# First-norm stage of a hybrid pool/RG-LRU block: x asked for ahead of its weights, squares spread over the blocks

## The chip, the cores and the metric

The kernel runs on one core of one Trainium2 chip. The metric is the device time of one execution in microseconds (us); lower is better. The engines are named as the profile names them: PE (TensorE; PEld is its weight load), DVE (VectorE), ACT (ScalarE), POOL (GpSimd) and SP (SyncE, which here issues nearly all transfers). Each engine works through its own instruction queue in order, and waits on semaphores that other engines and finished transfers raise.

## What is computed

One layer of a decoder trunk on x (1024 tokens, 1024 channels), float32. What matters for this change is the very first part:

```python
z = rms_norm(h, norm_mix_g[l])          # h is x
proj = z @ w_in[l]                       # 1024 -> 512 pool, 512 lru, 512 gate
u_pool, u_lru, u_gate = split(proj)
xb = causal_depthwise_conv(u_lru, ...)   # then RG-LRU, times gelu(u_gate)
y_pool = multiscale_pool_mixer(u_pool, pool_w, pool_b, pool_scale)
h = h + concat(y_pool, y_lru) @ w_out
...                                      # squared-ReLU MLP, gated per-layer embedding, final norm
```

`rms_norm` is `x * rsqrt(mean(x*x) + eps) * g`. The RG-LRU needs softplus of a parameter vector (`lru_L`), a small side computation.

## The kernel before, in words

Everything is held transposed: channels on the 128 partitions, the 1024 tokens along the free axis. The 1024 channels of x are eight blocks `H[0]` to `H[7]` of 128 x 1024 (512 KB each); in the text, "block k" is the step that treats `H[k]`.

Matrix products are made of float32 values that are split in two float32r parts, hi and lo, so that one product is three matmul passes: hi x hi, hi x lo, lo x hi. The helper `split` (L174) does this with one ACT instruction for hi (L177 without a gain, L180 with the gain of the norm) and one DVE instruction for lo (L178 or L181). The scaling by the inverse root comes after the product (L535), so the product can start before the sum of squares is known.

The change lies in the loop over the eight blocks (L489 to L522). Block k needs:

- its x: a transfer of `H[k]` (L495), and its split into `A[k]` hi and lo (L501, that is L180 on ACT and L181 on DVE);
- its weights: 128 x 384 of `w_lru` (192 KB), the columns of the first three output tiles, transferred into a raw buffer (L195) and split (L177 on ACT, L178 on DVE) by `load_weights`. Here these are called weights k, named `wl` in the profile. Raw, hi and lo buffers come from a pool of two (`wp`, bufs=2), so weights k+2 take the buffers of weights k: their hi part can be written once the last matmul that reads hi of weights k has ended, and their transfer can start once raw of weights k has been split;
- 18 matmuls 128 x 128 x 512 (L521 for blocks 2 to 7): three output tiles, three passes, two halves of the tokens;
- its square on ACT (L387 for the first, L390 for the others) and the addition to the running sum `T[0]` on DVE (L391), by `norm.add`. The squares go to two buffers in turn.

Around the loop stand side works: `tables` (L443, a small table on DVE and the transfers of the gate and pool weights, L452 and L453, 256 KB each) and `softplus` (L459, some 27 DVE instructions on 128 x 4 elements, most of which depend on the one before, and one exponential on ACT, L466). After block 6's matmuls come four matmuls that add up the squares over the partitions (`norm.sums`, L417 and L418), then those of block 7, and then the projections `ps_i`.

What sets the order: the program is written in the order of the source, and a scheduler of the tile framework may move instructions, except those that were pinned. `pin` (L169) pins an instruction to the source's order as long as the list `in_order` is not empty; `split` and `norm.add` pin their instructions. The list is cleared at L509, in block 2. `weights()` (L337) asks for the next weights of a long list (`ask`, L332: transfer and split) and returns the oldest that were asked for. In block 3 one more `ask()` (L492) stands ahead, so from there on the weights are one block ahead: block 4 asks for weights 5, block 5 for weights 6, and so on.

Of the kernel before, what the change touches and what calls it, by code (L numbers as in the profile page):

```python
# [14 lines left out]
S = 1024  # L15
# [7 lines left out]

SOON = 20

AHEAD = ((0,), (1, 2), (3,), ())
IN = {("P5", 2): (0, 1), ("P5", 3): (2, 3), ("P3", 0): (4, 5), ("P3", 1): (6, 7)}
LATER = ((), (0, 1), (2, 3), (4, 5), (6, 7), (), ())
# [29 lines left out]
def block_kernel(  # L58
# [26 lines left out]
    H = [h_all[:, i] for i in range(NT)]  # L85
# [44 lines left out]
    HALVES = FIRST, SECOND = slice(0, HALF), slice(HALF, S)  # L130
# [14 lines left out]
    def f32(ap):  # L145
        return ap.bitcast(F32)
# [16 lines left out]
    def col(name, i):  # L163
        c = COLS[name] + i
        return vecs[:, c : c + 1]
# [3 lines left out]
    def pin(ins):  # L169
        return tc.keep_in_program_order(ins) if in_order else ins  # L170
# [3 lines left out]
    def split(src, hi, lo, g=None, eng=None):  # L174

        if g is None:
            first = pin(nc.scalar.activation(hi, src, AF.Copy))  # L177
            lowest[:] = [pin((eng or nc.vector).tensor_tensor(lo, src, f32(hi), ALU.subtract)).ins]  # L178
        else:
            first = pin(nc.scalar.activation(hi, src, AF.Identity, scale=g))  # L180
            lowest[:] = [pin(nc.vector.scalar_tensor_tensor(lo, src, g, f32(hi), ALU.mult, ALU.subtract)).ins]  # L181
        return first.ins

    def raw_tile(name):
        return wp.tile([P, S], F32, tag="raw", name=f"{name}_raw")

    def weight_tiles(name):
        return [wp.tile([P, S], F32R, tag=f"w{x}", name=f"{name}_{x}") for x in ("hi", "lo")]
# [143 lines left out]
    def ask():  # L332
        if todo:
            fn, *args = todo.pop()
            asked.append(fn(*args))

    def weights():  # L337
        ask()
        return asked.pop(0)

    def mm(parts, whi, wlo, zhi, zlo, first, last, only=None, more=False, held=False):
        outs = [
            (slice(hs.start + n, hs.start + min(n + HALF, w)), ps[:, n : min(n + HALF, w)])
            for hs, ps in parts
            for w in (hs.stop - hs.start,)
            for n in range(0, w, HALF)
            if only is None or hs.start + n == only.start
        ]
        for w, z in ((whi, zhi), (whi, zlo), (wlo, zhi)):
            for hs, ps in outs:  # L350
                ins = nc.tensor.matmul(  # L351
                    ps, w, turns(z[:, hs]),
                    start=first and z is zhi and w is whi,
                    stop=last and w is wlo,
                    skip_group_check=more,
                )
                if held:
                    tc.keep_in_program_order(ins)
                    held = False

    def kblk(t, k):
        return t[:, k * P : (k + 1) * P]
# [80 lines left out]
    def tables():  # L443

        one = ones_f[:, :16]
        tc.keep_in_program_order(
            nc.vector.tensor_tensor_scan(recip_t, one, one, 0.0, ALU.mult, ALU.add)
        )
        nc.vector.reciprocal(recip_t, recip_t)


        nc.sync.dma_start(T[5][:, FIRST], gates)  # L452
        nc.sync.dma_start(T[5][:, SECOND], pool_w)  # L453
# [5 lines left out]
    def softplus():  # L459

        c0 = COLS["lru_l"]
        lv = vecs[:, c0 : c0 + NLRU]
        with tc.issue_after(lowest[0]):
            nc.vector.tensor_scalar_mul(neg, lv, -1.0)
        nc.vector.tensor_tensor(e, lv, neg, ALU.max)
        nc.scalar.activation(e, e, AF.Exp, scale=-1.0)  # L466
        nc.vector.tensor_scalar_add(s, e, 2.0)
        nc.vector.reciprocal(s, s)
        nc.vector.tensor_tensor(s, s, e, ALU.mult)
        nc.vector.tensor_tensor(s2, s, s, ALU.mult)  # L470
        nc.vector.memset(poly, 1.0 / 19)
        for n in range(8, -1, -1):
            nc.vector.tensor_tensor(poly, poly, s2, ALU.mult)
            nc.vector.tensor_scalar_add(poly, poly, 1.0 / (2 * n + 1))
        nc.vector.tensor_tensor(poly, poly, s, ALU.mult)
        nc.vector.tensor_scalar(neg, neg, 0.0, 8.0, ALU.max, ALU.mult)
        nc.vector.scalar_tensor_tensor(cpos, poly, 16.0, neg, ALU.mult, ALU.add)
        nc.vector.tensor_scalar_mul(cneg, cpos, -1.0)

        c_b, c_s = COLS["pool_b"], COLS["pool_s"]  # L480
        with tc.issue_after(lowest[0]):
            nc.vector.tensor_tensor(pool_bs, vecs[:, c_b : c_b + NPOOL], vecs[:, c_s : c_s + NPOOL], ALU.mult)

    norm = Norm("n0", T[0], T[1:3])
# [2 lines left out]
    for _ in range(WARM):  # L487
        nc.tensor.matmul(ps_l[2][0][1][:, :HALF], heat, wide, start=True, stop=True)
    for k in range(NT):  # L489
        if k:  # L490
            if k == 3:
                ask()  # L492
            whi, wlo = weights()
        for hs in HALVES if k < 2 else (slice(0, S),):
            nc.sync.dma_start(H[k][:, hs], xT[k * P : (k + 1) * P, hs])  # L495
            if k == hs.start == 0:
                raw = raw_tile("wl0")[:, : 3 * P]
                whi, wlo = (t[:, : 3 * P] for t in weight_tiles("wl0"))
                nc.sync.dma_start(raw, w_lru[:P, :])
                pin(nc.vector.tensor_copy(whi, raw))  # L500
            split(H[k][:, hs], A[k][0][:, hs], A[k][1][:, hs], col("g_mix", k))  # L501
            if k == hs.start == 0:
                pin(nc.vector.tensor_tensor(wlo, raw, f32(whi), ALU.subtract))
        if k == 2:
            norm.add(H[0])
            norm.add(H[1])
        if k > 1:
            norm.add(H[k])
            in_order.clear()  # L509
        if k == 2:  # L510
            tables()
            softplus()
        if k == NT - 1:
            norm.rstd(R)
        if k < 2:

            for hs in HALVES:
                for o in range(3):
                    mm(ps_l[o], kblk(whi, o), kblk(wlo, o), *A[k], k == 0, False, hs)
            continue  # L520
        for o in range(3):  # L521
            mm(ps_l[o], kblk(whi, o), kblk(wlo, o), *A[k], False, k == NT - 1)  # L522
# [159 lines left out]
    norm = Norm("n1", T[4], T[5:])  # L682
# [66 lines left out]
    def add_got(to, ps, y=None):  # L749

        add(by(to, ps), got(ps), None if y is None else by(y, ps))
# [155 lines left out]
    def prepare(n, tp):  # L907

        if n < NOPS:
            split(X[tp], *A[4 * (n % 2) + tp])  # L910
            load_x(n + 1, tp)
# [19 lines left out]
    def down(n):  # L931
# [6 lines left out]
        for q in range(NQ):  # L938
# [36 lines left out]
            else:  # L975
                add_got(c12, x)
            for tp in AHEAD[q] if n else AHEAD[q - 1]:
                prepare(n + 1, tp)
# [252 lines left out]
```

## Time and profile before

| | |
|---|---|
| time, median of 3 runs (lowest to highest) | 930.12 us (929.95 to 930.37) |
| the profiled execution: time, span | 930.07 us, 928.2 us |
| granted TensorE clock | 0.998 |
| PE busy | 916.3 us (99%) |
| DVE busy | 765.9 us (83%) |
| ACT busy | 457.4 us (49%) |
| POOL busy | 14.9 us (2%) |

The time is what the runs are compared by; the span is the profiled stretch inside it, 1.87 us shorter in this execution. In a row of the timeline the first number is the start in us from the span's start, the second the duration in us, then the engine, the line of the kernel, the operation, output<-input, the shapes and the count (x2: two instructions merged into one row, from the start of the first to the end of the last). Square brackets name the idle time just before and what ended it. SPq is the issue of a transfer on SP's queue, not the transfer itself. Instructions of one engine overlap a little: the next often starts before the end that is shown for the one before, so the distance of two starts is the better price of an instruction in a row of others. Ends of matmuls are modelled.

### The profile page before, as it was taken

To read this page: it belongs to the slowest core of one execution; us is meant where nothing else is said; L and a number is where in the kernel's file an instruction comes from. 1 tells how busy PE (TensorE), PEld (TensorE's weight loads), DVE (VectorE), ACT (ScalarE), POOL (GpSimd) and SP (SyncE) were. 2 spreads that over 40 slices of the span, in tenths; PEclk is the share of its full clock that TensorE was granted. 3 is DMA by queue.
4 is the path that set the end of the run, shared out by engine and by line. 5 is a ranking of instruction groups with operands and counts; after the bars stand their busy time and mean duration, and the time that the engine had idled before them with its cause. 6 is when DMAs were issued, how large, how long until landed. Compare 5 with 4: busy or idle time off the path is not lost.

```text
span 928.2 us, 11481 instructions
## 1 busy us (share of the span) xinstructions
PE 916.3 (99%) x4471; PEld 802.4 (86%) x4471; DVE 765.9 (83%) x930; ACT 457.4 (49%) x545; POOL 14.9 (2%) x11
## 2 busy tenths in 40 slices
PE   9999999999999999999999999999999999999996
PEld 6888888888888888888888888888888888888995
DVE  6997984669998888888888989979776679885976
ACT  7567893447543343343334654434343446653445
POOL 0000000002000000000000000000000000000220
PEclk9999999999999999999999999999999999999999
DMA  7210143211254355345434988366522441031122
GB/s 264 96 50 23 46 154 118 68 45 67 72 189 161 125 175 197 126 148 178 174 125 153 361 314 315 128 209 203 186 91 91 136 136 46 24 117 43 46 92 91
DMA packets 45333, 125.03 MB, mean 135 GB/s; under 512 B 4192, under 2 KB 6240, under 8 KB 45280
## 3 DMA queue, kind: packets, MB, share of 16 engines
q1 hardware_dynamic: 45136, 124.27, 38.4%
q8 instruction: 35, 0.57, 0.3%
q14 instruction: 18, 0.15, 0.1%
q10 hardware_dynamic: 144, 0.04, 0.0%
HBM read 90.74 MB, written 33.55 MB: 134 GB/s over the span
## 4 chain that ended last, share of the span: by engine, by line
PE 91%; DVE 5%; ACT 2%; DMA 1%; issue 0%; DVEq 0%; ACTq 0%
PE ps_P_u L351 31%; PE ps_P_d L351 31%; PE ps_i L351 10%; PE ps_o L351 9%; PE ps_e L351 6%; PE ps_l L351 2%; DVE h L1062 1%; PE ps_j L351 1%; PE ps_g L571 1%; DMA wl_raw<-in_w_lru 1%; DVE h L1079 1%; PE ps_p L351 1%; DVE t L391 1%; DVE t L1061 0%; DVE t L1055 0%; DVE a L178 0%
## 5 line engine op out<-in xcount | busy, mean ns | idle before, releaser
L351 PE MATMUL ps_P_d<-a,wd_P_hi 128*128 128x512 f32 x880 | 261.7, 379 | 0.0
L351 PEld LDWEIGHTS ps_P_d<-a,wd_P_hi 128*128 128x128 f32 x880 | 166.3, 189 | 23.6
L351 PE MATMUL ps_P_d<-a,wd_P_lo 128*128 128x512 f32 x440 | 166.8, 379 | 0.0
L351 PE MATMUL ps_P_u<-a,wu_hi 128*128 128x512 f32 x512 | 152.3, 379 | 0.0
L351 PE MATMUL ps_P_u<-y,wu_hi 128*128 128x512 f32 x384 | 114.2, 379 | 0.0
L351 PEld LDWEIGHTS ps_P_u<-a,wu_hi 128*128 128x128 f32 x512 | 96.8, 189 | 13.8
L351 PE MATMUL ps_P_u<-a,wu_lo 128*128 128x512 f32 x256 | 97.0, 379 | 0.0
L351 PEld LDWEIGHTS ps_P_d<-a,wd_P_lo 128*128 128x128 f32 x440 | 83.2, 189 | 11.8
L351 PEld LDWEIGHTS ps_P_u<-y,wu_hi 128*128 128x128 f32 x384 | 72.6, 189 | 10.3
L747 DVE TENSOR_TENSOR t<-t,ps_P_u 128x512 f32<-128x512 f32 (+1 forms) x80 | 62.6, 783 | 20.4 <-PE ps_P_u L351 20.4
L351 PE MATMUL ps_i<-a,wi_hi 128*128 128x512 f32 x288 | 74.3, 380 | 0.0
L351 PE MATMUL ps_P_u<-y,wu_lo 128*128 128x512 f32 x192 | 72.8, 379 | 0.0
L177 ACT ACTIVATE a<-wd 128x1024 fp32r<-128x1024 f32 x56 | 59.0, 1055 | 21.6 <-PE ps_P_d L351 11.6
L178 DVE TENSOR_TENSOR a<-wd,a 128x1024 fp32r<-128x1024 f32 x56 | 67.4, 1223 | 1.3 <-ACT a L177 0.9
L351 PE MATMUL ps_o<-y,wo_hi 128*128 128x512 f32 x256 | 65.7, 379 | 0.0
L351 PEld LDWEIGHTS ps_i<-a,wi_hi 128*128 128x128 f32 x288 | 54.1, 189 | 8.8 <-issue 0.7
L177 ACT ACTIVATE wu_hi<-wu 128x1024 fp32r<-128x1024 f32 x24 | 25.4, 1059 | 69.8 <-PE ps_P_u L351 44.1
L177 ACT ACTIVATE wu_hi<-wu_raw 128x1024 fp32r<-128x1024 f32 (+1 forms) x26 | 25.3, 976 | 66.3 <-PE ps_P_u L351 41.3
L351 PEld LDWEIGHTS ps_o<-y,wo_hi 128*128 128x128 f32 x256 | 48.4, 189 | 6.8
L351 PEld LDWEIGHTS ps_P_u<-a,wu_lo 128*128 128x128 f32 x256 | 48.4, 189 | 6.8
L177 ACT ACTIVATE wd_P_hi<-wd 128x1024 fp32r<-128x1024 f32 x24 | 25.3, 1055 | 47.3 <-PE ps_P_d L351 47.2
L390 ACT ACTIVATE t<-h 128x512 f32<-128x512 f32 (+2 forms) x47 | 32.8, 699 | 28.9 <-DVE h L1062 20.1
(226 smaller groups left out, 1540.6 us busy)
## 6 DMA issues: line engine op xcount, KB each, us to landing
wd<-act SPq DMA_DIRECT2D x56, 512.0 KB, 5.6
act<-t SPq DMA_DIRECT2D x32, 512.0 KB, 4.3
wu_raw<-in_w_up SPq DMA_DIRECT2D x16, 512.0 KB, 3.2
wu<-in_w_up SPq DMA_DIRECT2D x16, 512.0 KB, 3.8
act<-wu SPq DMA_DIRECT2D x16, 512.0 KB, 4.6
wd<-in_w_down SPq DMA_DIRECT2D x16, 512.0 KB, 6.3
h<-in_xT SPq DMA_DIRECT2D x14, 512.0 KB, 4.5
wg_raw<-in_w_gate SPq DMA_DIRECT2D x12, 512.0 KB, 3.2
```

What stands on the lines that cost most here:

```text
L177: first = pin(nc.scalar.activation(hi, src, AF.Copy))
L178: lowest[:] = [pin((eng or nc.vector).tensor_tensor(lo, src, f32(hi), ALU.subtract)).ins]
L351: ins = nc.tensor.matmul(ps, w, turns(z[:, hs]), start=first and z is zhi and w is whi, stop=last and w is wlo, skip_group_check=more,)
L390: pin(nc.scalar.activation(sq, t[:, hs], AF.Square))
L391: self.eng.tensor_tensor(self.acc[:, hs], self.acc[:, hs], sq, ALU.add)
L571: nc.tensor.matmul(x, w[r, o * P : (o + 1) * P], turns(z[r, at : at + HALF]), start=n == 0, stop=n == 2)
L747: (eng or nc.vector).tensor_tensor(to, to if y is None else y, x, ALU.add)
L1062: nc.vector.tensor_tensor(hv, hv, e, ALU.add)
L1079: nc.vector.scalar_tensor_tensor(hv, hv, col("g_fin", o), rfin[:, hs], ALU.mult, ALU.mult)
```

## The change

In the loop, for blocks 2 to 7, the transfer of `H[k]` is issued ahead of the request for the weights (before, it stood behind it). The additional `ask()` moves from block 3 to block 4. The squares are spread by a table: those of blocks 0 and 1 move behind the splits of blocks 2 and 3, and blocks 4, 5 and 6 add those of blocks 2 and 3, 4 and 5, and 6; block 7 adds its own. The pinned stretch now ends in block 6. `softplus` stays in block 2 but no longer follows `tables`, which moves to block 3, so that the transfers of the gate and pool weights come behind that of the fourth block of x. No arithmetic changes.

```diff
+AFTER = (), (), (0,), (1,), (2, 3), (4, 5), (6,)
...
     for k in range(NT):
-        if k:
-            if k == 3:
-                ask()
+        halves = HALVES if k < 2 else (slice(0, S),)
+        if k == 1:
             whi, wlo = weights()
-        for hs in HALVES if k < 2 else (slice(0, S),):
+        for hs in halves:
             nc.sync.dma_start(H[k][:, hs], xT[k * P : (k + 1) * P, hs])
             if k == hs.start == 0:
                 raw = raw_tile("wl0")[:, : 3 * P]
                 whi, wlo = (t[:, : 3 * P] for t in weight_tiles("wl0"))
                 nc.sync.dma_start(raw, w_lru[:P, :])
                 pin(nc.vector.tensor_copy(whi, raw))
+            if k > 1:
+                if k == 4:
+                    ask()
+                whi, wlo = weights()
             split(H[k][:, hs], A[k][0][:, hs], A[k][1][:, hs], col("g_mix", k))
             if k == hs.start == 0:
                 pin(nc.vector.tensor_tensor(wlo, raw, f32(whi), ALU.subtract))
-        if k == 2:
-            norm.add(H[0])
-            norm.add(H[1])
-        if k > 1:
-            norm.add(H[k])
+        for i in AFTER[k] if k < len(AFTER) else (k,):
+            norm.add(H[i])
+        if k == 6:
             in_order.clear()
         if k == 2:
+            softplus()
+        if k == 3:
             tables()
-            softplus()
         if k == NT - 1:
             norm.rstd(R)
```

## The prediction

> **What bounds the kernel now.** I read the page first (busy shares, chain of waits), then the timeline of each engine over the first 42 us, then the transfers' times to landing. From the page:
>
> ```profile
> span 928.2 us, 11481 instructions
> PE 916.3 (99%) x4471; PEld 802.4 (86%) x4471; DVE 765.9 (83%) x930; ACT 457.4 (49%) x545; POOL 14.9 (2%) x11
> ...
> PE 91%; DVE 5%; ACT 2%; DMA 1%; issue 0%; DVEq 0%; ACTq 0%
> ```
>
> PE is busy 99% of the span and is 91% of the chain. So the change is worth what it does to the moment at which PE ends the block loop: PE has no slack behind it in which a delay could vanish, and an early finish is passed on whole. PE's timeline of the loop:
>
> ```profile
> 1.05 4.02 PE L488 MATMUL ps_l<-heat 128*128 128x512 bf16 x9 [1.05 <-DVE heat L368]
> ...
> 18.01 0.59 PE L351 MATMUL ps_l<-a,wl_hi 128*128 128x512 f32 x2
> 19.36 0.70 PE L351 MATMUL ps_l<-a,wl_hi 128*128 128x512 f32 x2 [0.76 <-DVE a L181]
> ...
> 22.92 1.03 PE L351 MATMUL ps_l<-a,wl_hi 128*128 128x512 f32 x4
> ...
> 26.80 1.03 PE L351 MATMUL ps_l<-a,wl_hi 128*128 128x512 f32 x4
> ...
> 30.69 1.03 PE L351 MATMUL ps_l<-a,wl_hi 128*128 128x512 f32 x4
> ...
> 34.57 0.40 PE L417 MATMUL n_ps<-hl,ones 128*128 128x512 f32 x1
> ...
> 35.51 1.03 PE L351 MATMUL ps_l<-a,wl_hi 128*128 128x512 f32 x4
> ...
> 39.39 1.03 PE L351 MATMUL ps_i<-a,wi_hi 128*128 128x512 f32 x4
> ```
>
> Blocks 3, 4, 5, 6 start at 18.01, 22.92, 26.80 and 30.69, the sums of squares at 34.57, block 7 at 35.51; 39.39 is the end of the loop. A block without a stall takes 3.88 us (22.92 to 26.80), 0.2155 per matmul. There is one stall: block 3 takes 4.91 us, 1.03 too much, because lo of x 3 (DVE L181) came late; 0.76 of it is shown as idle time, the rest is the slower restart. That is all the loop can give back: 0.11% of the time, less than the 0.2% (1.9 us) that a measurement of this kernel can tell from no change.
>
> **The change part by part.** The rows that price it, ACT first, then DVE:
>
> ```profile
> 13.76 1.99 ACT L390 ACTIVATE t<-h 128x1024 f32<-128x1024 f32 x2
> 15.65 0.19 ACT L466 ACTIVATE sp<-sp 128x4 f32<-128x4 f32 x1
> 15.75 0.51 ACT L177 ACTIVATE wl_hi<-wl_raw 128x384 fp32r<-128x384 f32 x1
> 16.16 1.14 ACT L180 ACTIVATE a<-h,vecs 128x1024 fp32r<-128x1024 f32 x1
> 17.21 1.04 ACT L390 ACTIVATE t<-h 128x1024 f32<-128x1024 f32 x1
> 18.16 1.13 ACT L180 ACTIVATE a<-h,vecs 128x1024 fp32r<-128x1024 f32 x1
> ...
> 30.51 0.53 ACT L177 ACTIVATE wl_hi<-wl_raw 128x384 fp32r<-128x384 f32 x1 [2.39 <-PE ps_l L351]
> 34.34 1.06 ACT L177 ACTIVATE wi_hi<-wi_raw 128x1024 fp32r<-128x1024 f32 x1 [3.31 <-PE ps_l L351]
> ```
>
> ```profile
> 14.34 0.16 DVE L465 TENSOR_TENSOR sp<-vecs,sp 128x4 f32<-128x4 f32 x1
> 14.53 0.17 DVE L476 TENSOR_SCALAR sp<-sp 128x4 f32<-128x4 f32 x1
> 14.83 1.23 DVE L391 TENSOR_TENSOR t<-t 128x1024 f32<-128x1024 f32 x1
> 15.98 0.16 DVE L467 TENSOR_SCALAR sp<-sp 128x4 f32<-128x4 f32 x1
> 16.09 1.23 DVE L391 TENSOR_TENSOR t<-t 128x1024 f32<-128x1024 f32 x1
> ...
> 18.03 1.27 DVE L181 SCALAR_TENSOR_TENSOR a<-h,vecs,a 128x1024 fp32r<-128x1024 f32 x1
> 19.22 0.16 DVE L470 TENSOR_TENSOR sp<-sp 128x4 f32<-128x4 f32 x1
> ...
> 20.50 0.55 DVE L178 TENSOR_TENSOR wl_lo<-wl_raw,wl_hi 128x384 fp32r<-128x384 f32 x1
> 20.97 0.17 DVE L474 TENSOR_SCALAR sp<-sp 128x4 f32<-128x4 f32 x1
> ...
> 32.55 0.44 DVE L415 CAST hl<-t 128x512 fp32r<-128x512 f32 x1
> ...
> 33.36 0.70 DVE L416 TENSOR_TENSOR hl<-t,hl 128x512 fp32r<-128x512 f32 x1
> ```
>
> From start to start, ACT takes 0.41 for a weight hi, 1.05 for an x hi, 0.95 for a square; DVE 1.19 for an x lo, 0.47 for a weight lo, 1.26 for an addition behind the one it depends on, 0.19 for a dependent softplus step. All the work stays; only its order changes. In the built program the queues behind block 3 now stand so: ACT: hi of weights 4, x 7, weights 5, x 4, squares 2 and 3, weights 6, x 5, squares 4, 5 and 7, weights 7, x 6, square 6. Before, every x hi stood ahead of the weight hi that waits. Up to block 2's matmuls (end 18.01) nothing moves.
>
> *Block 3.* Two squares leave the place at 13.76, so the exponential starts at 14.55 (behind L465), hi of weights 3 at 14.65, hi of x 3 at 15.07 to 16.20. Its data are there: x 3 is asked for where the gates were (6.21 instead of 9.67, rows below). On DVE five softplus steps from 14.88 on come first, then lo of weights 3 at 15.75, ended 16.31, four more steps, and lo of x 3 at 16.9, ended 18.17. PE needs it at 18.44: the stall goes. Block 3 ends at 21.89. **-1.03 us.**
>
> *Block 4.* ACT's queue has hi of x 7 ahead of weights 5 and x 4, since block 7's split is not pinned and was moved up. It waits for the transfer of x 7, which on SP's queue stands behind that of weights 5, and that waits for lo of weights 3 (16.31). So weights 5, x 6 and x 7 are issued at 16.35, 16.7 and 17.2. The landing times of x before (issue, then the three single transfers of x 4, x 5 and x 7):
>
> ```profile
> 6.21 0.65 SPq L452 DMA_DIRECT2D t<-in_gates  x1
> ...
> 9.67 0.43 SPq L495 DMA_DIRECT2D h<-in_xT  x1
> 12.48 0.33 SPq L195 DMA_DIRECT2D wl_raw<-in_w_lru  x1
> 12.86 1.38 SPq L495 DMA_DIRECT2D h<-in_xT  x3
> ```
>
> ```profile
> h<-in_xT SPq DMA_DIRECT2D x1, 512.0 KB, 4.6
> ```
>
> ```profile
> h<-in_xT SPq DMA_DIRECT2D x1, 512.0 KB, 6.3
> ```
>
> ```profile
> h<-in_xT SPq DMA_DIRECT2D x1, 512.0 KB, 4.8
> ```
>
> The first of the three issued at 12.86 took 4.6, the second 6.3; x 7, almost alone, 4.8. The new x 7 is the second behind a weight transfer, as the 6.3 was, but with no third beside it: I take 5.8, landing at 23.0, with 21.8 and 23.5 as ends. Then hi of x 7 from 23.05, of weights 5 at 24.09, of x 4 from 24.50 to 25.64: PE starts block 4 at 25.70 instead of 21.89. **+3.81.** DVE brings lo of x 7 (24.22), weights 5 (25.41) and x 4 (25.88 to 27.16). PE now runs the six hi x hi matmuls first (25.70 to 27.10 with the restart), waits a trace for lo, and ends at 29.92: **+0.34** over 3.88.
>
> *Block 5.* Its x hi stands behind hi of weights 6, which takes the buffer of weights 4 and waits for block 4's last hi matmul. The rows at 30.51 and 34.34 show when such a wait ends: 0.18 and 0.23 ahead of the next start on PE (30.69, 34.57), say 0.2. So: 29.72, plus 0.41, plus 1.14 for hi of x 5, plus 0.06: PE starts at 31.33, a stall of **1.41**, and **0.11** for the restart (as at 19.36). Its lo (31.31 to 32.6) is ready within the first six matmuls. End: 35.32.
>
> *Block 6.* The same 1.52, and more: ahead of weights 7 stands square 7, which overwrites square 5's buffer. DVE adds square 4 from 32.50 and square 5 from 33.76 to 34.99; square 7 starts at 35.03, hi of weights 7 at 35.98, of x 6 from 36.39 to 37.53. PE starts at 37.59, a stall of **2.27**, plus **0.11**, and ends at 41.58.
>
> *Sums and block 7.* Its x and weights are long there. But the sums need squares 6 and 7 added (DVE 38.8 to 41.3), two casts (0.44) and two lo parts (0.70), between which lo of the next weights stands, and PE's queue has these four matmuls among block 7's. I count three short waits with restarts: **+0.7** (0.2 if the casts win the race, 1.2 if hi of the next weights holds DVE up).
>
> *Behind the loop* the order is nearly the old one; DVE's first scaling (40.50 before) follows PE's loop end by some half us more, which a block's slack hides; if not, it is half a us more. The moved gate and pool transfers are covered: their first reader is the split at the sums. Softplus' end on DVE falls in the wait for x 7.
>
> Sum: -1.03 + 3.81 + 0.34 + 1.52 + 2.38 + 0.7 = **+7.7 us**. On the profiled execution's 930.07 this is 937.8; the median of the runs (930.12) differs by 0.05, which changes nothing.
>
> **The clock.** The nine warm-up matmuls at 1.05 took 0.447 each for the 512 columns that later cost 0.2155: PE starts slow. The idle 0.76 us ahead of 19.36 brought no slow stretch back. [...] The stall ahead of block 4 is forecast at 3.8 us, five times the one seen. If it cools PE, block 4's first nine matmuls cost 9 x 0.23 = 2.1 us more, by the first row.
>
> **The rivals.** (a) *x 7 lands early* (by 20.6): then hi of x 7 fits in ACT's wait for block 3's last hi matmul, block 4 starts at 21.69 + 0.41 + 1.14 + 0.06 = 23.30, 2.4 us sooner: 935.4. For it: fewer bytes are in flight than before at 12.86; against: it would need 3.4 us, and the shortest landing shown for 512 KB of x is 4.6. (b) *PE cools* at block 4: 939.9, as worked out. (c) *Not slower*: the weight buffers come free early enough that x hi of blocks 4 to 6 is ready in time, and only the gain at block 3 is left: 929.0. For it: DVE and ACT have the time, and data arrive earlier. Against: hi of x k stands behind hi of weights k+1 on ACT, and that reads a semaphore that only block k-1's 16th matmul raises. It decides only if x 7, x 4, x 5 and x 6 cost together under 2.9 us of stall; two bounded stalls of 1.5 already use that up.
>
> **How the numbers follow.** Forecast as summed 65% (own range 936.3 to 939.0, from 21.8 to 23.5 for x 7 and the 0.2 to 1.2 of the sums); (a) or between 15%; (b) 12%; (c) 5%; something else 3%. Range 935.0 to 940.2: it leaves out (c) and the tails. Faster by over 0.2%: 1%, since the loop has only 1.03 to give; within 0.2%: 5%, case (c); slower: 94%.
>
> **What would show it.** Right: in the profile after, PE's block 3 without idle time; then idle times of about 3.8, 1.4 and 2.3 us ended by ACT x hi (L181 there), and 46 to 48 us as the start of `ps_i`; ACT idle on the transfer of x once, and on PE ahead of weight hi. Wrong: block 4 starting at 23.3 or earlier, matmuls at 0.43 behind the stall, or no idle time on PE ahead of blocks 5 and 6.

## The result and the profile after

| | before | after |
|---|---|---|
| median (lowest to highest) | 930.04 us (929.83 to 930.37), 4 runs | 938.95 us (938.44 to 941.30), 4 runs |
| the profiled execution: time, span | 930.07 us, 928.2 us | 941.30 us, 939.5 us |
| granted TensorE clock in it | 0.998 | 0.992 |

The ratio is 1.0103, with a 95% interval of 1.0088 to 1.0118: the kernel became slower by 8.9 us. The prediction was 937.8, with a range of 935.0 to 940.2. The profiled execution of after is the slowest of its four, 2.4 us above the median, so a second profiled execution of the same kernel (938.33 us, below called "after, again") is read beside it. The page of after:

```profile
span 939.5 us, 11488 instructions
PE 920.3 (98%) x4471; PEld 804.0 (86%) x4471; DVE 767.7 (82%) x930; ACT 457.4 (49%) x545; POOL 15.2 (2%) x11
```

PE has as many matmuls as before, and four microseconds more of busy time (920.3 against 916.3): work that is the same took longer. The rest of the 11.3 us by which the span grew is idle time. PE's timeline of the block loop shows both (starts in us, duration, and in brackets the idle time ahead and what ended it):

```profile
17.58 1.03 PE L352 MATMUL ps_l<-a,wl_hi 128*128 128x512 f32 x4
...
21.04 0.59 PE L352 MATMUL ps_l<-a,wl_lo 128*128 128x512 f32 x2
26.06 3.78 PE L352 MATMUL ps_l<-a,wl_hi 128*128 128x512 f32 x8 [4.43 <-ACT a L181]
29.64 1.06 PE L352 MATMUL ps_l<-a,wl_lo 128*128 128x512 f32 x2
...
32.10 0.59 PE L352 MATMUL ps_l<-a,wl_lo 128*128 128x512 f32 x2
33.91 2.02 PE L352 MATMUL ps_l<-a,wl_hi 128*128 128x512 f32 x8 [1.22 <-ACT a L181]
...
40.24 2.73 PE L352 MATMUL ps_l<-a,wl_hi 128*128 128x512 f32 x8 [2.15 <-ACT a L181]
...
50.93 1.03 PE L352 MATMUL ps_i<-a,wi_hi 128*128 128x512 f32 x4
```

Block 3 runs without a break from 17.58 to 21.47 (two matmuls behind 21.04, 0.2155 each). Blocks 4, 5 and 6 each begin with an idle time that ACT's hi of x ends. The loop ends at 50.93 where it ended at 39.39. The same eight matmuls that open a block take 2.02 in block 5, but 3.78 in block 4 and 2.73 in block 6. The same places in the timeline of after, again:

```profile
20.60 0.59 PE L352 MATMUL ps_l<-a,wl_lo 128*128 128x512 f32 x2
23.82 2.75 PE L352 MATMUL ps_l<-a,wl_hi 128*128 128x512 f32 x8 [2.63 <-ACT a L181]
...
30.91 2.02 PE L352 MATMUL ps_l<-a,wl_hi 128*128 128x512 f32 x8 [1.22 <-ACT a L181]
...
37.23 2.51 PE L352 MATMUL ps_l<-a,wl_hi 128*128 128x512 f32 x8 [2.15 <-ACT a L181]
...
47.95 1.03 PE L352 MATMUL ps_i<-a,wi_hi 128*128 128x512 f32 x4
```

Here the first stall is 1.8 us shorter. The other two are equal to the hundredth, and the eight slow matmuls in blocks 4 and 6 are there again. ACT's timeline of after says who holds hi of x up:

```profile
17.40 0.52 ACT L178 ACTIVATE wl_hi<-wl_raw 128x384 fp32r<-128x384 f32 x1 [0.71 <-PE ps_l L352]
23.41 1.15 ACT L181 ACTIVATE a<-h,vecs 128x1024 fp32r<-128x1024 f32 x1 [5.49 <-DMA h<-in_xT]
24.46 0.51 ACT L178 ACTIVATE wl_hi<-wl_raw 128x384 fp32r<-128x384 f32 x1
24.88 1.13 ACT L181 ACTIVATE a<-h,vecs 128x1024 fp32r<-128x1024 f32 x1
...
32.30 0.52 ACT L178 ACTIVATE wl_hi<-wl_raw 128x384 fp32r<-128x384 f32 x1 [4.39 <-PE ps_l L352]
32.73 1.13 ACT L181 ACTIVATE a<-h,vecs 128x1024 fp32r<-128x1024 f32 x1
...
37.68 1.06 ACT L391 ACTIVATE t<-h 128x1024 f32<-128x1024 f32 x1 [1.92 <-DVE t L392]
38.64 0.51 ACT L178 ACTIVATE wl_hi<-wl_raw 128x384 fp32r<-128x384 f32 x1
39.05 1.13 ACT L181 ACTIVATE a<-h,vecs 128x1024 fp32r<-128x1024 f32 x1
```

At 23.41 stands hi of x 7, which block 4 does not need, after 5.49 us of waiting for its transfer; hi of x 4 follows at 24.88, and PE starts 1.18 later. At 32.30 hi of weights 6 has waited for PE, and hi of x 5 comes behind it. At 37.68 square 7 has waited for DVE, and hi of weights 7 and of x 6 come behind that.

The clock is read from PE's busy time by stretches of 3.41 us, cut at the moments at which the granted clock changes in the trace. The columns are: stretch, its length, busy time of PE, PEld, DVE, ACT and POOL with the instructions in it, the granted clock, the DMA share, GB/s. After:

```profile
20.87:24.28 3.41, 0.76 (x4) 0.33 (x2) 1.07 (x7) 0.87 (x1) 0.00 (x0) 1.00 0.28 94
24.28:27.69 3.41, 1.63 (x4) 1.35 (x5) 3.10 (x4) 3.41 (x5) 0.00 (x0) 0.50 0.11 20
27.69:31.11 3.42, 3.42 (x10) 2.69 (x9) 2.21 (x2) 0.21 (x1) 0.00 (x0) 0.50 0.14 45
...
37.94:41.35 3.41, 1.26 (x6) 1.01 (x6) 1.69 (x2) 3.19 (x4) 0.00 (x0) 1.00 0.18 59
41.35:44.76 3.41, 3.41 (x10) 2.61 (x9) 3.34 (x6) 0.00 (x0) 0.00 (x0) 0.50 0.25 95
```

The same cut for after, again:

```profile
21.55:24.96 3.41, 1.14 (x5) 1.03 (x6) 2.76 (x4) 3.41 (x5) 0.00 (x0) 1.00 0.05 17
24.96:28.38 3.42, 3.42 (x9) 2.51 (x9) 2.70 (x3) 0.71 (x1) 0.00 (x0) 0.50 0.24 62
28.38:31.79 3.41, 2.19 (x10) 1.60 (x10) 1.46 (x2) 2.50 (x4) 0.00 (x0) 1.00 0.12 29
...
35.20:38.62 3.42, 1.39 (x6) 1.12 (x7) 1.97 (x3) 2.92 (x4) 0.00 (x0) 1.00 0.25 65
38.62:42.03 3.41, 3.41 (x9) 2.76 (x9) 3.34 (x5) 0.00 (x0) 0.00 (x0) 0.50 0.23 89
```

In both traces the changes of the clock in the loop lie one, two or three such stretches apart. A stretch in which PE was busy for 0.76, 1.14, 1.26 or 1.39 us is followed by one at half clock; one with 2.19 (in the second of the two views) is not. In after, again, blocks 4 and 6, each with one half-clock stretch, took 5.70 us, and block 5, at full clock behind its stall, 4.01: a half-clock stretch that PE filled cost 1.7 us there, half its length. None of the four stretches ahead of a fall was idle throughout: PE was busy for up to 1.39 us of one.

### The profile page after: what moved, and what is told of

The parts are those of the page before. It is cut to its first block, busy times and chain, and to the rows that moved or that the text cites. A ratio compares the mean times of both kernels' runs of the same rounds, so it can differ in the third digit from the quotient of the medians.

```text
span 939.5 us, 11488 instructions
## 1 busy us (share of the span) xinstructions
PE 920.3 (98%) x4471; PEld 804.0 (86%) x4471; DVE 767.7 (82%) x930; ACT 457.4 (49%) x545; POOL 15.2 (2%) x11
## 4 chain that ended last, share of the span: by engine, by line
PE 90%; DVE 5%; ACT 2%; DMA 1%; issue 1%; DVEq 0%; ACTq 0%
PE ps_P_d L352 31%; PE ps_P_u L352 31%; PE ps_i L352 10%; PE ps_o L352 9%; PE ps_e L352 6%; PE ps_l L352 2%; DMA wl_raw<-in_w_lru 1%; DVE h L1065 1%; DVE t L392 1%; PE ps_j L352 1%; PE ps_g L574 1%; DVE h L1082 1%; PE ps_p L352 1%; ACT a L181 1%; DVE t L1064 0%
```

## The experiments

The kernel before was run beside each group: 929.61 us beside the first four, 929.48 beside the next four, 929.36 beside the last three. Ratios are against it, with their 95% intervals.

The theory: three things keep hi of x from PE, namely hi of x 7 ahead of hi of x 4 on ACT, hi of the next weights ahead of hi of x, and a clock that fell to half behind the longer stalls (4.43 and 2.15 us of idle time in after, 2.63 and 2.15 in after, again). The rivals: the transfers' new order is the cause; or the squares' places on ACT and DVE are; or the slow matmuls are something other than the idle time ahead of them.

**Split of x 7 behind that of x 6.** Its square and the request for block 7's weights come behind it, and the pinned stretch reaches to there.

```diff
-            if k > 1:
+            if 1 < k < NT - 1:
                 ...
             split(H[k][:, hs], A[k][0][:, hs], A[k][1][:, hs], col("g_mix", k))
+            if k == NT - 1:
+                norm.add(H[k])
+                in_order.clear()
+                whi, wlo = weights()
-        for i in AFTER[k] if k < len(AFTER) else (k,):
+        for i in AFTER[k] if k < len(AFTER) else ():
             norm.add(H[i])
-        if k == 6:
-            in_order.clear()
```

> As the changed kernel, but the pinned stretch ends in block 7: the split and the square of x 7 stand behind those of x 6, and the weights that block 7 asks for come behind them. Theory (ACT's queue order): block 4 no longer waits for the transfer of x 7, but x hi of blocks 4, 5 and 6 still stands behind a weight hi that waits for its buffer. So PE stalls about 1.4 us ahead of each of the three blocks, block 6 loses its extra 0.8, no stall is long enough to cool PE. Time: 930.05 - 1.0 + 3 x 1.5 + 0.7 = 934.2 us, no stretch of half clock inside the loop. Rival (late data: x and weights themselves land too late): the stall ahead of block 4 stays at 4 us or more and the time at 937 or above. Rival (the clock alone): without a cool stretch the time is back at 930.

Measured: 933.39 us (933.20 to 933.71), ratio 1.0038 (1.0023 to 1.0052). PE's timeline of this kernel:

```profile
23.14 2.02 PE L352 MATMUL ps_l<-a,wl_hi 128*128 128x512 f32 x8 [1.22 <-ACT a L181]
...
28.54 2.02 PE L352 MATMUL ps_l<-a,wl_hi 128*128 128x512 f32 x8 [1.22 <-ACT a L181]
...
33.94 2.02 PE L352 MATMUL ps_l<-a,wl_hi 128*128 128x512 f32 x8 [1.22 <-ACT a L181]
...
43.04 1.24 PE L352 MATMUL ps_i<-a,wi_hi 128*128 128x512 f32 x4
```

Blocks 4, 5 and 6 now start 5.40 us apart, 1.52 over a block without a stall, and none of them runs at half clock. Three times 1.52, less 1.03 for block 3, plus 0.27 (the sums and block 7 take 5.09 from 37.95, against 4.82) are 3.8; measured are 933.39 - 929.61 = 3.78. So the price of "weights ahead of x" on ACT is settled at 1.52 a block. The place of x 7 and of its square, with the cooled clock, is the other 5.1 to 5.4 us of after. The square's share is 0.9: block 6's stall was 2.3 us in after, and is 1.4 here.

**The split of x ahead of the request for weights**, on top of the last, in blocks 2 to 6:

```diff
+            split(H[k][:, hs], A[k][0][:, hs], A[k][1][:, hs], col("g_mix", k))
             if 1 < k < NT - 1:
                 if k == 4:
                     ask()
                 whi, wlo = weights()
-            split(H[k][:, hs], A[k][0][:, hs], A[k][1][:, hs], col("g_mix", k))
```

> As x7_behind, and in blocks 2 to 6 the split of x stands ahead of the request for the weights, so x hi no longer stands behind a weight hi that waits for its buffer. Transfers are asked for in the same order as in the changed kernel. Theory (queue order): no stall ahead of blocks 3 to 6; the loop ends about 1 us earlier than in the kernel before: 929.1 us, 930 if the sums of squares, which now wait for the squares of blocks 6 and 7 at the very end, cost 0.7 to 1. Rival (late data): stalls of over 1 us ahead of blocks 4 to 6 remain, ended by transfers, 933 or more. Rival (the additions of the squares and softplus on DVE hold lo back): PE's stalls are ended by DVE x lo, 931 to 933.

Measured: 930.17 us (929.84 to 930.60), ratio 1.0005 (0.9996 to 1.0015). No stall by ACT is left. What is left came by the way of the last rival, though not at its price: PE's timeline has a stall by DVE, at lo of x 5:

```profile
27.45 0.70 PE L352 MATMUL ps_l<-a,wl_hi 128*128 128x512 f32 x2 [0.85 <-DVE a L182]
```

DVE's timeline at that place:

```profile
23.66 2.55 DVE L392 TENSOR_TENSOR t<-t 128x1024 f32<-128x1024 f32 x2
26.12 1.28 DVE L182 SCALAR_TENSOR_TENSOR a<-h,vecs,a 128x1024 fp32r<-128x1024 f32 x1
```

Two additions to the sum of squares stand ahead of that lo. So with both orders mended on ACT the change costs nothing that can be measured, and gains nothing: the stall of block 3 has become one of block 5, ended by the same kind of instruction.

**Own buffers for weights 5, 6 and 7.** Their hi and lo go to tiles that are free until later, so that hi of the next weights waits for no matmul, though it still stands ahead of hi of x on ACT. (The split of x 7, still unpinned, falls behind that of x 4 here.)

```diff
-        hi, lo = (t[:, :width] for t in weight_tiles(name))
+        if name in ("wl5", "wl6", "wl7"):
+            hi, lo = (t[:, :width] for t in B[int(name[2]) - 5])
+        else:
+            hi, lo = (t[:, :width] for t in weight_tiles(name))
```

> As the changed kernel, but hi and lo of weights 5, 6 and 7 go to buffers of their own (tiles that lie idle until the convolution), so that their hi part waits for no matmul. Raw buffers and transfers as before; x 7 is still moved up, now behind squares 2 and 3. Theory (the buffer is what the weight hi waits for): block 4 starts with at most a short wait for the transfer of weights 5, blocks 5 and 6 lose at most some tenths to the wait for x 7 in ACT's queue: 929.5 to 931.5 us. Rival (late data): 933 or more with ACT waiting for transfers ahead of x 4 and x 5. If the stalls of 1.4 and 2.2 us ahead of blocks 5 and 6 are there as before, the buffer is not their cause.

Measured: 931.56 us (931.12 to 931.85), ratio 1.0020 (1.0010 to 1.0029), just above the range expected. PE's timeline, where `y` is the tile that now holds these weights:

```profile
28.26 9.22 PE L355 MATMUL ps_l<-a,y 128*128 128x512 f32 x40 [1.25 <-DVE a L182]
```

No stall by hi of x is left here either. What is left is DVE, above all with lo of x 5, after 1.25 us of idle time: lo of x 7, which is still moved up, starts on DVE at 25.66, right ahead of lo of x 5 at 26.93. So hi of weights ahead of hi of x costs PE nothing if it need not wait: the wait, not ACT's 0.41 us of work, is the price. The early split of x 7 costs something even where its transfer holds nobody up, namely its 1.27 us on DVE, which has no room.

**Matmuls in the gap.** After, with 13 matmuls of constants (bfloat16, 128 x 512, into a bank that is free then) placed on PE behind block 3; they add nothing to the result.

```diff
+FILL = 13
...
+    early_bank = []
...
+        if k == 3:
+            early_bank.append(bank("n0_ps0"))
+            for _ in range(FILL):
+                tc.keep_in_program_order(
+                    nc.tensor.matmul(early_bank[0], heat, wide, start=True, stop=True)
+                )
```

> As the changed kernel, with 13 additional matmuls of constants on PE behind block 3 (2.8 us of the stall ahead of block 4 that the trace shows as 4.4 us), written to the bank that the sums of squares clear later. Nothing else moves. Theory (two parts: the stall itself, and PE cooled by it): the stall's end stays where it is, about 4.6 us behind the end of block 3, but the idle time falls to about 1.8 us and blocks 4 to 6 run at 0.2155 us per matmul: 938.45 - 2.4 = 936.0 us, and single executions no longer reach 941. Rival (the slow stretch has another cause, such as contention or the restart): still half clock in block 4, 938 to 939. Rival (the stall is only waiting of PE's own making): block 4 starts later by the filler's 2.8 us, 941.

Measured: 936.31 us (936.24 to 937.87), ratio 1.0073 (1.0058 to 1.0088). PE's timeline of this kernel:

```profile
21.22 2.98 PE L533 MATMUL n_ps<-heat 128*128 128x512 bf16 x13
24.22 0.92 PE L354 MATMUL ps_l<-a,wl_hi 128*128 128x512 f32 x3
```

Hi of x 4 comes no earlier than in after, again (block 4 at 24.22, there 23.82), but PE, kept at work, runs block 4 at full clock: it takes 4.87 us (24.22 to 29.09, 0.62 of it a wait for lo), against 5.70 in after, again. In this trace the clock does not fall in block 6 either, though the 2.15 us of idle time are the same. The kernel is 2.5 us faster than after (6.7 us above its before, against 9.2). In after, again, blocks 4 and 6 take 5.70 us each, where block 5, at full clock behind a stall, takes 4.01: the half clock costs 3.4 us there. Block 4's 4.87 us, with a wait for lo that half clock had hidden, take back 0.9 of them.

**After, again.** The changed kernel without an edit, for a second trace.

> The changed kernel once more, for a second trace of it and a time beside the others of this call. Theory: the transfer of x 7 lands between 21.5 and 23.4 us (the filler run showed the early end, the first trace the late one), so the stall ahead of block 4 is 3 to 4.5 us of idle time; stalls of 1.2 and 2.2 us ahead of blocks 5 and 6 as in the first trace; a stretch of half clock in block 4 and, in this execution, perhaps none in block 6. Time 938.0 us, 937.5 to 939.5. If x 7 lands early and PE still runs at half clock in block 4, an idle time of about 3 us is enough for it.

Measured: 938.69 us (937.31 to 939.79), ratio 1.0099 (1.0084 to 1.0114). Its rows stand in the section on the result: a first stall of 2.63 us of idle time, shorter than the 3 to 4.5 expected, and half clock in both places. The landing of x 6 and x 7, issued together, explains the first stall's size. SP's timeline of after has their issue, and the transfers' view the median of the two from issue to landing:

```profile
16.20 0.91 SPq L495 DMA_DIRECT2D h<-in_xT  x2
```

```profile
h<-in_xT SPq DMA_DIRECT2D x2, 512.0 KB, 6.3
```

The same for after, again, with hi of x 7 on ACT:

```profile
15.76 0.91 SPq L495 DMA_DIRECT2D h<-in_xT  x2
```

```profile
h<-in_xT SPq DMA_DIRECT2D x2, 512.0 KB, 4.1
```

```profile
21.17 1.15 ACT L181 ACTIVATE a<-h,vecs 128x1024 fp32r<-128x1024 f32 x1 [3.68 <-DMA h<-in_xT]
```

X 7 is the second of the two, issued 0.48 behind the first: at 16.68 and at 16.24. ACT starts its hi at 23.41 and at 21.17, so it took about 6.7 and 4.9 us, at the same place of the queue in two executions of one kernel.

**The transfers' new order alone.** The squares' table and the long pinned stretch are taken out of after; x ahead of its weights, `ask()` in block 4 and `tables` in block 3 stay.

```diff
-        for i in AFTER[k] if k < len(AFTER) else (k,):
-            norm.add(H[i])
-        if k == 6:
+        if k == 2:
+            norm.add(H[0])
+            norm.add(H[1])
+        if k > 1:
+            norm.add(H[k])
             in_order.clear()
```

> The changed kernel without its squares: x ahead of its weights, the extra request in block 4 and the gate and pool weights behind the fourth block as in the change, but the squares of blocks 0 to 2 in block 2 and the pins ended there, as in the kernel before. ACT's queue is then the same as before. Theory (the loss comes from what the longer pinned stretch makes of ACT's queue): no stalls ahead of blocks 4 to 6, the stall inside block 3 stays, since ACT does the squares first: 929.6 us, as before, within 0.5. Rival (the other order of the transfers is the cause): 932 or more.

Measured: 929.45 us (929.00 to 930.03), ratio 1.0000 (0.9991 to 1.0009). PE's timeline has the old stall, a little shorter:

```profile
19.02 0.70 PE L352 MATMUL ps_l<-a,wl_hi 128*128 128x512 f32 x2 [0.53 <-DVE a L182]
```

The order of the transfers alone is worth nothing, either way: x 3 comes earlier, but lo of x 3 was late because of the additions and softplus steps that DVE does ahead of it.

**The squares' table and the long pinned stretch alone**, put into the kernel before:

```diff
+AFTER = (), (), (0,), (1,), (2, 3), (4, 5), (6,)
...
-        if k == 2:
-            norm.add(H[0])
-            norm.add(H[1])
-        if k > 1:
-            norm.add(H[k])
+        for i in AFTER[k] if k < len(AFTER) else (k,):
+            norm.add(H[i])
+        if k == 6:
             in_order.clear()
```

> The kernel before with nothing but the squares of the change: spread over the blocks, pins up to block 6. Transfers in the old order, the extra request in block 3, so that hi of weights 4 now stands ahead of x 3 as well. Theory (queue order): four stalls instead of three: about 1.2 us idle ahead of block 3, then 3 to 4.5 (x 7 is moved up here too), 1.2 and 2.2, with half clock behind the long one: 938 to 941 us. Rival (the transfers' order is the cause): 930.

Measured: 937.11 us (936.60 to 939.07), ratio 1.0087 (1.0070 to 1.0104). PE's timeline:

```profile
19.46 1.56 PE L352 MATMUL ps_l<-a,wl_hi 128*128 128x512 f32 x6 [1.27 <-ACT a L181]
...
37.09 2.02 PE L352 MATMUL ps_l<-a,wl_hi 128*128 128x512 f32 x8 [2.15 <-ACT a L181]
```

The damage is here: this part alone costs 7.6 us, where the whole change costs 8.9 to 9.2. It is not made of the same pieces, though, and the expectation missed one. The same 2.15 us appear, and two stalls of 1.22, and hi of x 3 is held up too, by the weights that block 3 asks for here. But the long stall ahead of block 4, expected at 3 to 4.5 us, is only one of the 1.22: hi of x 7 waits for its transfer here too, and starts on ACT at 22.50, while PE still works on the late block 3. The loop has no half clock in this trace, although one idle time is 2.15 us long; the section on the prediction says why.

**The pinned stretch cut at block 3.** The transfers of after; squares 0 to 3 behind the split of x 3, no pins from there on.

```diff
-        for i in AFTER[k] if k < len(AFTER) else (k,):
-            norm.add(H[i])
-        if k == 6:
+        if k == 3:
+            norm.add(H[0])
+            norm.add(H[1])
+            norm.add(H[2])
+        if k > 2:
+            norm.add(H[k])
             in_order.clear()
```

> A try at the gain: transfers as in the changed kernel, squares 0 to 2 behind the split of x 3, pins ended in block 3. ACT's queue is x 3, squares 0 to 2, weights 4, square 3, x 4, square 4, x 5, weights 5 and on, so no x hi stands behind a weight hi that waits for a younger block. Theory: block 3 runs without a stall (-1.0), block 4 may lose 0.5 to 1.3 to its lo, which stands behind three additions on DVE: 928.6 to 930.0 us. Rival: 932 or more if x hi is late again.

Measured: 930.97 us (930.65 to 931.81), ratio 1.0018 (1.0009 to 1.0027). The expectation missed by 1 us. Block 3 has no stall, and lo of x 4 comes late, as was thought possible:

```profile
23.76 0.70 PE L352 MATMUL ps_l<-a,wl_hi 128*128 128x512 f32 x2 [0.96 <-DVE a L182]
```

In DVE's timeline the additions moved behind lo of x 3 stand ahead of lo of x 4. The stall goes wherever the additions go. In this trace block 4 takes 1.23 us over 3.88, and the sums with block 7 take 0.67 over 4.82, 0.27 of it as idle time; less the 1.02 that block 3 gains, the loop is 0.9 us longer. The trace is of the fastest of the ten executions, and what else is in the 1.5 us of the medians is not seen.

**A longer gap of known length.** The kernel with x 7 behind has three stalls of 1.22 us and no half clock. One or two squares of x 0, which nothing reads, are put on ACT between hi of weights 5 and hi of x 4, so that only block 4's stall grows, by about 1 us each (to 2.17 and 3.25).

```diff
+PAD = 2
...
                 whi, wlo = weights()
+                if k == 4:
+                    for _ in range(PAD):
+                        pin(nc.scalar.activation(T[3], H[0], AF.Square))
```

> x7_behind with two additional squares of x 0 on ACT (into a scratch tile that nothing reads) between hi of weights 5 and hi of x 4: the stall ahead of block 4 grows by 1.9 us, from 1.2 to about 3.1 us of idle time, with no transfer in it. Question: what idle time cools PE. By the traces of the changed kernel, in which 2.0 to 2.7 us idle inside one stretch of 3.41 us were each time followed by half clock: block 4 or 5 holds a stretch of half clock in nearly every execution, 933.4 + 1.9 + 1.2 to 2 = 936.5 to 937.3 us. If only 3.4 us or more of unbroken idle time cools PE, no stretch of half clock and 935.3 us.

Measured with two: 937.18 us (936.99 to 938.12), ratio 1.0084 (1.0071 to 1.0098). PE's timeline:

```profile
24.87 3.54 PE L353 MATMUL ps_l<-a,wl_hi 128*128 128x512 f32 x8 [3.25 <-ACT a L182]
```

Busy times by stretches, cut at the change of the clock:

```profile
21.19:24.60 3.41, 0.43 (x2) 0.02 (x1) 1.31 (x6) 3.35 (x4) 0.00 (x0) 1.00 0.40 128
24.60:28.01 3.41, 3.14 (x7) 2.52 (x8) 3.05 (x3) 2.11 (x3) 0.00 (x0) 0.50 0.03 5
```

With no transfer involved, idle time alone brings the half clock. The kernel is 3.8 us slower than the one without the two squares (4.0, each against its own before): 2.0 for the longer stall, and 1.8 to 2.0 for the clock. In the trace block 4 takes 5.53 us, 1.5 more than behind a short stall.

With one square (`PAD = 1`):

> The same with one additional square: the stall ahead of block 4 grows by 0.95 us to about 2.2 us. By the traces so far PE cools if over some 2.0 us of it fall in one stretch of 3.41 us, which runs freely: some executions at 934.3, others 1 to 2 us above, so a wider scatter than x7_behind's 0.5. If half clock needs 3.4 us idle: 934.3 us with the narrow scatter.

Measured: 935.15 us (934.35 to 936.10), ratio 1.0061 (1.0047 to 1.0075). The four executions lie apart: 934.35 and 934.52 at a mean granted clock of 0.997 and 0.998, 935.79 and 936.10 at 0.996 each. The first pair is 1.0 to 1.1 above the kernel without the square, which is the square; the second pair is 1.3 to 1.75 above the first, which would be about one half-clock stretch. The profiled execution was of the first pair, so the stretch itself was not seen for this kernel.

**A more even spread of the squares**, on top of the kernel with the split of x first, to see whether it can beat the kernel before:

```diff
-AFTER = (), (), (0,), (1,), (2, 3), (4, 5), (6,)
+AFTER = (), (), (0,), (1,), (2,), (3, 4), (5, 6)
```

> A second try at the gain: x_first with the squares spread more evenly (2 in block 4, 3 and 4 in block 5, 5 and 6 in block 6, 7 in block 7), so that one addition less stands ahead of lo of x 5 on DVE. Theory: x_first lost 0.85 us of idle time ahead of lo of x 5; that goes, the sums of squares wait as in x_first or 0.5 longer: 929.0 us against 929.5 of the kernel before, at best 1 us below it. Rival (the sums come too late and hold block 7 and the first projection up): 930 to 931.

Measured: 930.05 us (929.43 to 931.52), ratio 1.0008 (0.9999 to 1.0017). Lo of x 5 is in time now (PE had waited 0.85 us for it), and PE waits 0.17 us for lo of x 6. But the sums of squares end later, as the rival had it, and PE waits at the loop's end instead. PE's timeline:

```profile
39.41 0.67 PE L352 MATMUL ps_i<-a,wi_hi 128*128 128x512 f32 x2 [0.29 <-DVE rstd L436]
```

No version beat the kernel before. The one microsecond that the loop has to give went back and forth between the splits and the sums on DVE.

## Why the prediction was right, and where its steps were not

The time was right, at 938.95 against 937.8, and so were the direction and the cause of the three stalls: hi of x behind what waits on ACT. That the number came so near is in part luck. Behind it stand one term that hung on a landing time, a small one that was too large, and one, the clock, that was left to a rival and came. Each step by its length on PE, in us over the kernel before:

| step | predicted | after | after, again |
|---|---|---|---|
| block 3 | -1.03 | -1.02 | -1.02 |
| block 4: stall | +3.81 | +4.59 | +2.79 |
| block 4: its matmuls | +0.34 | +2.59 | +1.82 |
| block 5: stall and matmuls | +1.52 | +1.51 | +1.52 |
| block 6: stall | +2.27 | +2.32 | +2.31 |
| block 6: its matmuls | +0.11 | +1.79 | +1.82 |
| sums and block 7 | +0.7 | +0.20 | +0.20 |
| sum | +7.7 | +11.98 | +9.44 |

The columns of the runs are differences of starts in the timelines: block 4 of after, again, for example, starts 23.82 - (20.60 + 0.43) = 2.79 behind the end of block 3. The loop's end moved by 0.4 and 0.9 us less than these sums, since block 3 started at 17.58 and 17.14 where it was 18.01; the two executions of one kernel differ by 0.44 there, and whether any of it belongs to the change is not settled.

- *Block 3* was right to the hundredth. The earlier transfer does not bring the gain by itself: with the transfers' order alone 0.53 us of the stall stay. Whether the squares' move would is not shown, since with it alone the weights hold x 3 up.
- *Block 4's stall* had the right cause: the unpinned split of x 7, moved up on ACT and waiting for its transfer. Its size hung on one landing time, 5.8 taken, from 4.6 to 6.3. It was about 6.7 and about 4.9 in the two executions, issued at 16.68 and 16.24 where 17.2 was forecast. The term was mis-sized for both, in opposite directions; no row of the trace of before could have told which.
- *The clock* is the step that failed. The prediction gave the cooled PE at block 4 a chance of 12%, since 0.76 us of idle time had not brought it, and priced it at 2.1 us. It fell to half in both traces of after, and in block 6 too, behind 2.15 us, which the prediction did not consider: its 0.11 there was 1.8. Matmuls at 0.43 behind the stall were what the prediction itself gave as a sign of being wrong, and they came (the two at 29.64 in after show 1.06 together, where two at full clock show 0.59). The start of `ps_i`, forecast at 46 to 48, was 50.93 and 47.95. The matmuls in the gap, at -2.5 us, and the two squares, at about +2 for the clock, show that idle time is the cause.
- *The chance of 12%* was the author's estimate: no row of before shows how much idle time brings the half clock. In after, again, 2.0 us of it in one stretch of 3.41 us were enough (3.41 less the 1.39 of PE's work). The 0.34 was too small as well, which the half clock hid: at full clock, with the matmuls in the gap, block 4 took 4.87, that is 0.99 over 3.88.
- *Blocks 5 and 6*: the stalls of 1.41 and 2.27 were right within 0.05, and the kernel with x 7 behind shows three copies of the first.
- *Sums and block 7* cost 0.20, the lower end given: while PE ran block 6 at half clock, DVE had 1.7 us more to bring the casts. At full clock it was 0.27 in the kernel with x 7 behind and 0.29 with the matmuls in the gap, so most of the 0.7 was too much in any case.
- So in the execution of after, again, -1.02 (block 4's stall) and -0.5 (the sums) hide half of the +3.2 of the two cooled blocks (1.48 and 1.71 above their terms), and this is the luck. The sum came as near to the median as rival (b), 1.15 us below it and (b) 0.95 above, while the case on PE was that of (b).
- *The rivals*: (a) an early x 7 did not come in full; the stall of 2.79 in after, again, lies between the 1.4 that (a) needed and the forecast 3.81. (b) came, on top. (c) fell: the stalls by ACT came to 6.0 us of idle time or more.

**Why 2.15 us cooled PE in some traces only.** They were followed by half clock in both traces of after, and not with matmuls in the gap or with the squares alone. The place of the stretches can be read from the trace, since full clock is first recorded near the start and ends behind the last matmuls, and these changes lie on the same grid. In before they are at 6.681 and 924.866, 269 stretches of 3.4133 apart, in after at 3.803 and 935.642, 273 of them. With matmuls in the gap it rises at 4.695 and falls at 929.707, 925.012 apart; that is 271 stretches of 3.4133, and 3.4133 is also the 261st part of the 890.879 from 44.763 to 935.642 in after. Counted from there, the gap of 34.65 to 36.80 is cut at 35.41:

```profile
32.00:35.41 3.41, 2.65 (x13) 1.98 (x11) 2.10 (x2) 1.48 (x3) 0.00 (x0) 1.00 0.13 52
35.41:38.83 3.42, 2.03 (x9) 1.71 (x10) 2.60 (x3) 2.29 (x3) 0.00 (x0) 1.00 0.43 138
```

PE was busy for over 2 us of both stretches, and the clock stayed full. With the squares alone the gap is cut too, at 35.67, and PE was busy for 2.68 and 1.99. In after the same gap lies wholly inside one stretch, in after, again, all but 0.12 of it, and PE was busy for 1.26 and 1.39. The profiled execution with one square fits as well: its gap of 2.17 us is cut at 22.77, PE was busy for 2.21 and 2.45, and the clock stayed full.

**Left open:** whether the two slower executions with one square had their gap inside one stretch, since neither has a trace; why x 7 took 4.9 us in one execution and 6.7 in another; and whether the earlier start of block 3 belongs to the change.

## What to carry to other kernels

In an in-order queue, a split or a load for a later block costs the time that it waits, which can be many times what it takes (5.49 us of waiting for 1.05 of work on ACT here): put what the next matmuls need ahead of what waits for a buffer or a transfer, and see where a scheduler puts the instructions that are not pinned. When a forecast opens several gaps on a busy PE, add up PE's idle time per stretch of the clock (3.41 us here, of which 2.0 idle in one were enough, and a gap of 2.15 cut in two was not) rather than ask whether one gap is long enough. Before work is spread to remove a stall, see whether the engine that was late (here DVE, with lo and the additions) has the room: else the stall moves with the work.

## What the runs showed of the hardware

- The granted clock fell to half behind stretches of 3.41 us in which PE still worked for 0.43 to 1.39 us, and stayed full behind those with 1.99, 2.03 and 2.19. In the traces of before, of after and with matmuls in the gap, it changed from its first rise to its last fall only at whole multiples of 3.4133 us (269, 273 and 271 of them in all), and in the loop it came back behind stretches that PE filled for 3.14 us (two squares), 3.41 and 3.42 (after; after, again). Where between 1.39 and 1.99 the bound lies is not known from these runs. A gap of some 2.2 us was followed by full clock in the three traces in which this grid cut it in two (matmuls in the gap, the squares alone, one square), and by half clock in the two in which it lay in one stretch (after; after, again).
- In after, a half-clock stretch of 24.28 to 27.69 in which PE was busy for 1.63 us was followed by a second one: the gap of 4.43 us, from which PE came back at 26.06, late in the first, brought two stretches of half clock.
- Two transfers of 512 KB at the same place of the queue took 6.3 us in one execution of a kernel and 4.1 in another (medians of the two).
